# Twelve convolution blocks of a hybrid layer move from a filler stream into Winograd pairs

## The chip, the cores and the metric

The kernel runs on one core of one Trainium2 chip. The metric is the time of one execution on the device in microseconds (us). Times of several executions are given as a median with the lowest and the highest; the profile and the trace come from one further execution, whose own time is given with them.

## The reference, cut to what matters

One step of a one-layer encoder. A prompt of 1024 tokens and a sample of 64 tokens are treated together as T = 1088 columns. All projections of the first half come from one weight matrix; `[z | xBC | dt | q | k | v | g_ssm | g_att]` are its outputs.

```python
proj = _rmsnorm(x) @ w_in
z, xbc, dt, q, k, v, g_ssm, g_att = split(proj)
xbc = silu(causal_conv4(past, xbc) + bias)      # 4 taps per channel, 3072 channels
x_s, B, C = split(xbc)                          # 2048 + 4*128 + 4*128
y_s = ssd_scan(x_s, dt, B, C) ...               # 4 groups of 8 heads
o = diff_attention(q, k, v)                     # 8 heads, two softmaxes each
x += W_out(sig(g_ssm) * (y_s @ W_bs) + sig(g_att) * (o @ W_ba))
x += conv_ffn(rmsnorm(x))
```

The change concerns `xbc`: a projection from 1024 to 3072 channels, a causal convolution of width 4 along the tokens of each channel, and silu. In the kernel it is 24 blocks of 128 channels. Block f = 16 + g holds B of state-space group g, block 20 + g its C, and blocks 4g to 4g + 3 its x.

## The kernel before, in words

Every float32 product is made of three TensorE products of rounded parts: `w_hi * b_hi`, `w_hi * b_lo` and `w_lo * b_hi`. Activations lie as 128 channels (partitions) by tokens; a matmul takes a 128x128 weight part and 272 tokens (a quarter of T).

The stages, in order of time:

1. **Values and parts.** The input is normalised and split into high and low parts.
2. **Input pairs** (`in_pair`, L646, listed in `INPUT`, L81). Two weight blocks at a time are multiplied with Winograd's form of Strassen's scheme: the two blocks' 256 channels and the 1024 inputs and 1088 tokens are cut in two each way, and seven products of half size take the place of eight. Each product p is made for two column halves s, so a pair has 14 *steps* (p, s) of 4 k-parts times 3 matmuls, 12 matmuls each, 168 in all. Here 20 pairs run: q and k (4 pairs each), z (8) and four of the gate pairs. `pile` issues a step's matmuls into a PSUM bank; the result is read by ScalarE (`S.copy`, L698 and L708) or VectorE (additions of partial sums, L700, L702, L710), and `done` finishes a quarter (a quarter is 128 channels by 544 tokens, named by block r and token half c) with silu (z, L676), tanh or nothing (gates) or squares (q, k) and stores it. The seven weight parts of the *next* pair are made beside it: loads of four quarters, four additions on GpSimd (L573 to L579) and seven splits into high and low (`split`, a cast on ScalarE L429 and a subtraction on VectorE L430), at steps that `lefts_at` lists.
3. **Side jobs beside the pairs.** `take_turn` is called once in each step; it advances a list of generators, `running`, and starts new ones from `beside`: cached keys, the step sizes dt, and finishing of q and k (norm, rotation, splits). A count of its turns puts the end of the last of these jobs at step 5 of the 15th pair.
4. **Attention with a filler stream** (from about 560 us to 1112 us). 72 units `attend` (8 heads of 9 row blocks) each do score matmuls S (L1128, L1129), the maximum on VectorE (L1133, L1137), two exponentials on ScalarE (L1142), the subtraction of the two softmaxes on VectorE (L1144 to L1146), transposes T on TensorE (L1157), copies (L1162, L1164) and the product with the values (L1177). Between a unit's transposes and its value products, `fill(rate)` (L1041) takes work from the generator `stream` (L1028): plain blocks, `project` (L178), each of 4 column parts of 24 matmuls (8 k-parts times 3, L171 to L173), 96 matmuls in all. `ORDER` (L80) lists them: 24 convolution blocks (`conv_tiles`, L987) and 8 gate blocks. The filler is counted in portions of 363 columns; a column part counts 272/363 = 0.75 portions, a block 3.0. `fill(FIRST)` takes 4 portions before the first unit, and each unit takes `ATT_STEPS` = 1.12 portions more. What is left over, and then the branch products, is taken in the scan.
5. **Scan** of the state-space groups, with filler; then the branches, the output and the feed-forward half, which the change does not touch.

In `conv_tiles` the two column parts of a token half are copied from PSUM to `pre` (L1002), with three columns ahead of them for the past (GpSimd copies, L997, L999, L1004, L1013, L1014); ScalarE makes tap 0 with bias (L1017), VectorE the three others (L1019); tanh (L1020) and one more VectorE operation (L1021) make silu, since tanh shares a function table with the softmax's exponential. The result goes to `x_sc` in device memory (L1022), which the scan reads.

The order of instructions on each engine is made by a scheduler when the kernel is built: it takes the ready instruction that is earliest in the program, `tc.high_priority` lifts some, and `after(...)` or `tc.issue_after` forbids one to come before another. On the chip each engine then runs its list in order. PSUM has 8 banks: in the input pairs 7 of them take products in turn, in attention 2 take filler (`pm`), 4 scores and 2 transposes.

Of the kernel before, what the change touches and what calls it, by code (L numbers as in the profile page):

```python
# [9 lines left out]
F32 = mybir.dt.float32  # L10
R32 = mybir.dt.float32r
AF = mybir.ActivationFunctionType
ALU = mybir.AluOpType
# [4 lines left out]
P = 128  # L18
D = 1024
KT = D // P  # L20
TP, TS = 1024, 64
T = TP + TS
PAST = 512
WIDE = ((0, 384), (384, 384), (768, 320))
HT = T // 2
# [42 lines left out]
LAST = 200  # L68
FIRST = 4
IDLE = 12  # L70
ATT_STEPS = 1.12
SCAN_STEPS = 1.17
BRANCH_AT = 2

# [1 line left out]
def group(g):  # L76
    return 16 + g, 20 + g, *range(4 * g, 4 * g + 4)


ORDER = (("c", group(0)), ("g", (11, 10)), ("c", group(1)), ("g", (9, 8)), ("c", group(2)), ("c", group(3)), ("g", (3, 2)))  # L80
INPUT = [(k, i) for k in "qk" for i in range(4)] + [("z", i) for i in range(8)] + [("g", i) for i in (2, 3, 6, 7)]  # L81
Q_DONE = 3

O_MIX, O_FFN, O_CW, O_CB, O_SN, O_D = 0, 8, 16, 112, 136, 152
# [6 lines left out]
def hybrid_layer(ctx: ExitStack, tc: tile.TileContext, xT, xt, prm, cst, rope, wvd, win, wbs, wba, wout, wup, wdn,  # L91
# [32 lines left out]
    def col(o):  # L124
        return par[:, o : o + 1]
# [36 lines left out]
    def after(*names):  # L162
        pins = ExitStack()
        for n in names:
            pins.enter_context(tc.issue_after(seen[n].ins))
        return pins
# [316 lines left out]
    rows_l = tc.alloc_tile_pool(name="rl", bufs=1)  # L483
    rows_r = tc.alloc_tile_pool(name="rg", bufs=1, side="right")

    def row(tag, name, dt=F32):
        if tag in ("fa", "fs", "fu"):
            w = {"fa": KT * P, "fs": 4 * P, "fu": HT}[tag]
            return rows_l.tile([P, w], dt, name=name, tag=tag, bufs=IN_ROWS[tag])
        w = {"ss": T}.get(tag, HT)  # L490
        return rows_r.tile([P, w], dt, name=name, tag=tag, bufs=IN_ROWS[tag])

    def couple(t, n=2):
        return t[:, : n * QW].rearrange("p (a t) -> p a t", a=n)
# [124 lines left out]

    def blocks_of(n):  # L620
        kind, j = INPUT[n]
        return [win[FIRST_BLOCK[kind] + 2 * j + r] for r in range(2)]

    def plain_left(n):
# [21 lines left out]
    def in_pair(n):  # L646

        kind, j = INPUT[n]
        u1, u2 = row("fx" if n == 1 else "fu", "u1"), row("fu", "u2")
        banks, out = {}, {}  # L650

        def pile(key, p, s, start):
            if start:
                banks[key, s] = acc(W2[s])
            ps, w, b = banks[key, s], left[n][p], parts[PARTS[p], s]
            for k in range(4):
                c = slice(P * k, P * (k + 1))
                for i, (x, y) in enumerate(((0, 0), (0, 1), (1, 0))):
                    seen["mm"] = PE.matmul(ps, w[x][:, c], b[y][:, k], start=start and k == i == 0, stop=k == 3 and i == 2,
                                           skip_group_check=not start)  # L660
            return ps

        def to(r, c, s):

            if (r, c) not in out:
                out[r, c] = row("fp", "pre")
            a, w = O2[s], W2[s]
            return out[r, c][:, a : a + w]

        def done(r, c):  # L670
            cs = slice(HT * c, HT * (c + 1))
            t = out[r, c][:, :HT]
            f = 2 * j + r
            if kind == "z":
                with after("root"):
                    seen["silu"] = act(t, t, AF.Silu)  # L676
            elif kind == "g":
                if f >= KT:
                    act(t, t, AF.Tanh, scale=0.5)
            else:  # L680
                if kind not in squares:
                    squares[kind] = row("ss", "ss")
                ss = squares[kind][:, cs]
                if (kind, c) not in begun_squares:
                    begun_squares.add((kind, c))
                    act(ss, t, AF.Square)
                else:
                    sq = row("fc", "sq")[:, :HT]
                    act(sq, t, AF.Square)
                    V.tensor_tensor(out=ss, in0=ss, in1=sq, op=ALU.add)  # L690
            send(out={"z": z_sc, "q": q_r, "k": k_r, "g": g_sc}[kind][P * f : P * (f + 1), cs], in_=t)

        at = yield
        for _ in range(14):
            p, s = at
            us = cols(s)
            if p == 0:
                seen["copy"] = S.copy(u1[:, us], pile("a", p, s, True))  # L698
            elif p == 1:
                seen["read"] = V.tensor_tensor(out=u2[:, us], in0=pile("b", p, s, True), in1=u1[:, us], op=ALU.add)  # L700
            elif p == 3:
                seen["read"] = V.tensor_tensor(out=u1[:, us], in0=pile("b", p, s, False), in1=u1[:, us], op=ALU.add)  # L702
            else:
                r, c, key, start, u = {2: (0, 0, "a", False, None), 4: (1, 1, "c", True, u1), 5: (1, 0, "d", True, u1),
                                       6: (0, 1, "c", False, u2)}[p]
                ps = pile(key, p, s, start)
                if u is None:
                    seen["copy"] = S.copy(to(r, c, s), ps)  # L708
                else:
                    seen["read"] = V.tensor_tensor(out=to(r, c, s), in0=ps, in1=u[:, us], op=ALU.add)  # L710
                if s == 1:
                    ripe.append(lambda r=r, c=c: done(r, c))
            at = yield
# [1288 lines left out]
```

## Time and profile before

| | |
|---|---|
| median of 3 executions | 2408.86 us (2404.99 to 2409.06) |
| profiled execution: its time, its span | 2400.86 us, 2399.1 us |
| TensorE busy (matmuls), granted clock | 99% of the span, 0.998 |
| VectorE, ScalarE, GpSimd busy | 72%, 50%, 26% |

How to read the lines: PE is TensorE's matmuls and PEld its weight loads, DVE is VectorE, ACT ScalarE, POOL GpSimd, SP the engine that issues most DMAs. A line such as `L1019 DVE SCALAR_TENSOR_TENSOR cc<-pre,par,cc` is line 1019 of the kernel on VectorE writing tile `cc` from `pre`, `par` and `cc`; behind it stand the count, busy microseconds, the mean in nanoseconds, and idle time of the engine ahead of it with what ended it. A PE duration includes the pipeline, so the distance from start to start, not the duration, is what a matmul costs. A row of the window view gives the stretch, its length, and each engine's busy time (with the number of instructions).

### The profile page before, as it was taken

Reading aid. Unit: us, or ns where it says so; the run is one execution under the profiler, and the core shown is the slowest. Engines: PE = TensorE matmul, PEld = TensorE weight load, DVE = VectorE, ACT = ScalarE, POOL = GpSimd, SP = SyncE. Lnnn points to the kernel's source line nnn. Section 1 sums busy time; section 2 is a strip of 40 time slices with the busy share of each in tenths; the row PEclk is TensorE's granted clock in tenths of the full one; section 3 lists DMA queues with packets and bytes.
Section 4 is the critical chain, followed back from the end, with each engine's and each line's share of the span. In section 5 each row is a group of like instructions: output and inputs, shape, how many; then the busy total and the mean of one; then the engine's idle time right before and its main releaser. Section 6 shows DMA issues by size and latency. Waiting matters only on the chain.

```text
span 2399.1 us, 48662 instructions
## 1 busy us (share of the span) xinstructions
PE 2376.1 (99%) x18661; PEld 2306.1 (96%) x18661; DVE 1725.5 (72%) x2953; ACT 1197.8 (50%) x2592; POOL 623.0 (26%) x683
## 2 busy tenths in 40 slices
PE   9999999999999999999999999999999999999999
PEld 9999999999999999999899889999999999999999
DVE  4678987646858768884789886646866766767866
ACT  6344454425656656665666674334533443353432
POOL 0032444220100000001222220013254554453343
PEclk9999999999999999999999999999999999999999
DMA  7873868426555444435988956664124424357975
GB/s 248 273 243 135 275 214 310 165 105 205 158 160 161 148 141 138 143 114 183 360 272 287 333 192 207 197 211 139 63 82 159 148 96 160 124 182 220 253 189 120
DMA packets 288202, 450.58 MB, mean 188 GB/s; under 512 B 35865, under 2 KB 178082, under 8 KB 287970
## 3 DMA queue, kind: packets, MB, share of 16 engines
q1 hardware_dynamic: 259058, 388.39, 49.0%
q0 software_dynamic: 10176, 25.50, 5.0%
q10 hardware_dynamic: 18736, 33.59, 3.9%
q8 instruction: 147, 2.41, 0.4%
q14 instruction: 85, 0.70, 0.1%
HBM read 294.86 MB, written 152.50 MB: 186 GB/s over the span
## 4 chain that ended last, share of the span: by engine, by line
PE 56%; DVE 3%; DMA 1%; issue 1%; ACT 1%; SPq 0%; DVEq 0%; ACTq 0%
PE mx L1639 13%; PE mx L1821 6%; PE mm L1639 5%; PE mm L171 4%; PE mm L173 4%; PE mm L172 4%; PE mx L173 3%; PE mx L171 3%; PE mx L172 3%; PE mm L1821 2%; PE yi L1328 1%; PE stp L1340 1%; PE ye L1334 1%; PE po L1177 1%; PE tr L1307 1%
## 5 line engine op out<-in xcount | busy, mean ns | idle before, releaser
L171 PE MATMUL mm<-b,w_hi 128*128 128x272 f32 x1376 | 409.2, 297 | 0.0
L173 PE MATMUL mm<-b,w_lo 128*128 128x272 f32 x1376 | 404.0, 294 | 0.0
L172 PE MATMUL mm<-b,w_hi 128*128 128x272 f32 x1376 | 403.8, 294 | 0.0
L171 PEld LDWEIGHTS mm<-b,w_hi 128*128 128x128 f32 x1376 | 259.4, 188 | 7.2 <-issue 4.9
L172 PEld LDWEIGHTS mm<-b,w_hi 128*128 128x128 f32 x1376 | 259.4, 189 | 6.2 <-issue 4.9
L173 PEld LDWEIGHTS mm<-b,w_lo 128*128 128x128 f32 x1376 | 258.9, 188 | 3.9 <-issue 3.1
L1639 PE MATMUL mx<-m,w_hi 128*128 128x272 f32 x776 | 149.3, 290 | 1.5 <-ACT m L429 1.3
L430 DVE TENSOR_TENSOR wh<-w_f,wh 128x512 fp32r<-128x512 f32 (+1 forms) x156 | 149.1, 956 | 0.0
L1639 PE MATMUL mx<-n,wh 128*128 128x272 f32 x1056 | 141.2, 288 | 1.2 <-DVE u L1666 1.2
L1639 PEld LDWEIGHTS mx<-n,wh 128*128 128x128 f32 x1056 | 135.7, 188 | 1.4 <-DVE u L1666 1.4
L1142 ACT ACTIVATE p_t<-sc,mx 128x512 f32<-128x512 f32 (+6 forms) x144 | 106.0, 739 | 58.7 <-DVE mx L1133 35.0
L171 PE MATMUL mx<-b,w_hi 128*128 128x272 f32 x416 | 122.5, 295 | 1.6 <-ACT w_hi L156 1.1
L1639 PEld LDWEIGHTS mx<-m,w_hi 128*128 128x128 f32 x776 | 121.9, 188 | 2.0 <-ACT m L429 1.5
L172 PE MATMUL mx<-b,w_hi 128*128 128x272 f32 x416 | 122.0, 294 | 0.0
L173 PE MATMUL mx<-b,w_lo 128*128 128x272 f32 x416 | 120.1, 291 | 0.2 <-DVE w_lo L157 0.2
L573 POOL TENSOR_TENSOR ws<-w_f 128x512 f32<-128x512 f32 (+1 forms) x51 | 69.2, 1356 | 195.0 <-DMA w_f<-in_win_dram 94.0
L1019 DVE SCALAR_TENSOR_TENSOR cc<-pre,par,cc 128x544 f32<-128x544 f32 (+1 forms) x144 | 111.2, 772 | 8.2 <-ACT cc L1017 6.9
L157 DVE TENSOR_TENSOR w_lo<-w_f,w_hi 128x1024 fp32r<-128x1024 f32 (+1 forms) x74 | 91.1, 1232 | 31.3 <-ACT w_hi L156 30.7
L1639 PE MATMUL mx<-m,w_lo 128*128 128x272 f32 x388 | 112.0, 289 | 0.0
L1648 ACT ACTIVATE cc<-pre,par 128x544 f32<-128x544 f32 (+1 forms) x44 | 37.2, 845 | 148.0 <-DVE pre L1683 147.0
L429 ACT CAST wh<-w_f 128x512 fp32r<-128x512 f32 (+1 forms) x156 | 95.3, 613 | 28.7 <-POOL w_f L579 7.9
L156 ACT CAST w_hi<-w_f 128x1024 fp32r<-128x1024 f32 (+1 forms) x74 | 77.5, 1049 | 51.5 <-PE mm L172 28.4
(472 smaller groups left out, 7123.4 us busy)
## 6 DMA issues: line engine op xcount, KB each, us to landing
w_f<-in_win_dram SPq DMA_DIRECT2D x40, 512.0 KB, 3.6
w_f<-in_wup_dram SPq DMA_DIRECT2D x80, 256.0 KB, 2.6
w_f<-in_win_dram SPq DMA_DIRECT2D x76, 256.0 KB, 3.2
bc<-a_sc SPq DMA_DIRECT2D x32, 512.0 KB, 6.7
b<-y_sc SPq DMA_DIRECT2D x24, 544.0 KB, 9.3
h_sc<-hb SPq DMA_DIRECT2D x44, 272.0 KB, 2.1
ht<-h_sc SPq DMA_DIRECT2D x22, 544.0 KB, 4.7
t_sc<-ht SPq DMA_DIRECT2D x22, 544.0 KB, 2.9
```

The source lines that it names most:

```text
L156: S.copy(hi, w)
L157: V.tensor_tensor(out=lo, in0=w, in1=hi, op=ALU.subtract)
L171: PE.matmul(ps, a_hi, b_hi, start=i == 0, stop=False)
L172: PE.matmul(ps, a_hi, b_lo, start=False, stop=False)
L173: PE.matmul(ps, a_lo, b_hi, start=False, stop=i == n - 1)
L429: S.copy(hi, src)
L430: V.tensor_tensor(out=lo, in0=src, in1=hi, op=ALU.subtract)
L573: G.tensor_tensor(out=s1, in0=q21, in1=q22, op=ALU.add)
L1019: V.scalar_tensor_tensor(cc[:, :m], pre[:, i : i + m], cw(i), cc[:, :m], ALU.mult, ALU.add)
L1142: act(p_t[:n, :nk], sc[c][:n, :nk], AF.Exp, bias=mx[:n, c : c + 1], accum_out=dst)
L1639: PE.matmul(ps, w[x][:, c], b[y][:, k], start=start and k == i == 0, stop=k == 3 and i == 2, skip_group_check=not start)
L1821: PE.matmul(ps, w[y][:, c], b[z][:, k], start=start and k == j == 0, stop=k == n - 1 and j == 2, skip_group_check=not start)
```

## The change

The twelve convolution blocks of state-space groups 0 and 1 leave the filler stream and become six input pairs, two blocks each (`PAIRED`): (B0, C0), two pairs of x of group 0, and the same for group 1. They stand between the last six pairs of `INPUT` (z 6, z 7, gates 2, 3, 6, 7), one before each; the number of pairs goes from 20 to 26. The stream keeps groups 2 and 3 and the gates: 20 blocks instead of 32, and `ATT_STEPS` goes from 1.12 to 0.62.

In such a pair the quarters are written to `fx` rows (550 wide now instead of 544, as are the `fc` rows) behind three free columns; the last part of the second token half is written in two pieces around the sample's own past. When a quarter is there, `done` starts a generator `convolved` on `running`: a GpSimd memset or four small GpSimd copies and tap 0 on ScalarE in one turn, one VectorE tap in each of the next three, silu (ScalarE's Silu, with a scale of 2 since the taps' weights are halved) in the next, and in the next the store. The second token half of a block needs the first one's last columns, so (r, c) = (1, 1) waits for (1, 0) and starts three turns after it.

```diff
-ATT_STEPS = 1.12
+ATT_STEPS = 0.62
...
-ORDER = (("c", group(0)), ("g", (11, 10)), ("c", group(1)), ("g", (9, 8)), ("c", group(2)), ("c", group(3)), ("g", (3, 2)))
-INPUT = [(k, i) for k in "qk" for i in range(4)] + [("z", i) for i in range(8)] + [("g", i) for i in (2, 3, 6, 7)]
+PAIRED = ((16, 20), (0, 1), (2, 3), (17, 21), (4, 5), (6, 7))
+ORDER = (("c", group(2)), ("g", (11, 10)), ("c", group(3)), ("g", (9, 8)), ("g", (3, 2)))
+INPUT = [(k, i) for k in "qk" for i in range(4)] + [("z", i) for i in range(6)]
+INPUT += [x for i, y in enumerate([("z", 6), ("z", 7)] + [("g", j) for j in (2, 3, 6, 7)]) for x in (("c", i), y)]
...
+        w = {"ss": T, "fx": HT + 6, "fc": HT + 6}.get(tag, HT)
...
+            if kind == "c" and c == 1 and s == 1:
+                m = TP - HT - a
+                return [(0, out[r, c][:, d + a : d + a + m]), (m, out[r, c][:, d + a + m + 3 : d + a + w + 3])]
...
+        def convolved(r, c):
+            t, f = out[r, c], PAIRED[j][r]
+            n, m = (HT, HT) if c == 0 else (TP - HT, HT + 3)
+            if c == 0:
+                G.memset(t[:, 0:3], 0.0)
+            else:
+                G.tensor_copy(t[:, 0:3], out[r, 0][:, HT : HT + 3])
...
+            cc = row("fc", "cc", more=True)
+            with after("copy"):
+                act(cc[:, :m], t[:, :m], AF.Identity, bias=col(O_CB + f), scale=cw(0))
+            yield 1
+            for i in range(1, 4):
+                with after("read"):
+                    V.scalar_tensor_tensor(cc[:, :m], t[:, i : i + m], cw(i), cc[:, :m], ALU.mult, ALU.add)
+                yield 1
+            with after("root", "copy"):
+                seen["silu"] = act(cc[:, :m], cc[:, :m], AF.Silu, scale=2.0)
+            yield 1
+            rs = slice(P * f, P * (f + 1))
+            send(out=x_sc[rs, HT * c : HT * c + n], in_=cc[:, :n])
...
+            if kind == "c":
+                for x in {(0, 0): (0,), (1, 0): (0, 1), (0, 1): (1,), (1, 1): ()}[r, c]:
+                    running.append([1 + 3 * (r == 1 and x == 1), convolved(r, x)])
+                return
```

## The prediction on record

> **What bounds the kernel now.** I read the page first, then the window view cut at the stages that the change touches, then single pairs and single attention units in the timeline, and last what TensorE's transposes wait for.
>
> ```profile
> PE 2376.1 (99%) x18661; PEld 2306.1 (96%) x18661; DVE 1725.5 (72%) x2953; ACT 1197.8 (50%) x2592; POOL 623.0 (26%) x683
> ```
>
> ```profile
> core 0: us, PE busy (x) PEld busy (x) DVE busy (x) ACT busy (x) POOL busy (x), PEclk, DMA share, GB/s
> 1200.00:1300.00 100.00, 100.00 (x830) 90.51 (x829) 89.54 (x126) 65.23 (x154) 26.68 (x20) 1.00 0.77 261
> 380.00:440.00 60.00, 59.59 (x471) 59.13 (x471) 48.15 (x84) 27.21 (x53) 21.87 (x23) 1.00 0.85 285
> 560.00:1112.00 552.00, 550.10 (x4224) 527.49 (x4222) 413.07 (x817) 336.62 (x866) 43.39 (x120) 1.00 0.46 146
> 443.00:548.00 105.00, 105.00 (x836) 105.00 (x835) 44.81 (x83) 34.65 (x66) 22.15 (x18) 1.00 0.33 116
> ```
>
> ```profile
> L1157 PE MATMUL pt<-con,p_t x328: 221/272/329, 580.3 to 1108.3; 128*128 128x128 f32 x144, 64*128 64x64 f32 x16, 64*64 64x64 f32 x4
> ...
> its engine sat idle before it (us, times) until:
>   issue: 1.7, 9
>   PE sc L1128: 0.7, 2
> ```
>
> TensorE is the bound everywhere, at full granted clock: 1.9 us idle in 552 us of attention (third row), none in the last five light pairs (fourth row), and the 328 transposes of attention, asked what they wait for, name no other engine. So a matmul that goes away is time, as long as nothing else ends later. The fourth row also shows room beside a light pair: VectorE is busy for 44.8 of 105 us. The first two rows are the measure for a crowded VectorE: 89.5% and 80% busy, with TensorE idle for 0 of 100 and 0.4 of 60 us.
>
> **Matmuls removed and added.** The distance from start to start, in two light pairs and in a piece of filler inside attention:
>
> ```profile
> 460.27 0.42 PE L659 MATMUL mm<-t,w_hi 128*128 128x272 f32 x2
> ...
> 481.43 0.42 PE L659 MATMUL mx<-t,w_hi 128*128 128x272 f32 x2
> ...
> 502.58 0.42 PE L659 MATMUL mx<-t,w_hi 128*128 128x272 f32 x2
> ```
>
> ```profile
> 810.91 0.29 PE L171 MATMUL mm<-b,w_hi 128*128 128x272 f32 x1
> ...
> 813.17 0.29 PE L171 MATMUL mm<-b,w_hi 128*128 128x272 f32 x1
> ```
>
> A pair of 168 matmuls takes 21.15 us, 125.9 ns each. In the filler, 18 matmuls lie between the two starts: 2.26/18 = 0.1256 us. Twelve plain blocks are 12 x 96 = 1152 matmuls, 1152 x 0.1259 = 145.0 us out of attention; six pairs are 6 x 168 = 1008, 6 x 21.15 = 126.9 us into the input stage. The balance is 144 matmuls, **-18.1 us**. The counts are fixed by the code, so that the change might save no matmuls is no case. The Trainium skill, page "TensorE: Matmul & The Clock Gate", section "Back-to-back issue gap", gives an isolated gap of columns/2.4 + 2.5 ns, 115.8 ns for 272 columns; by it the balance would be an estimated 16.7 us. The trace's 125.9 ns decides.
>
> Nothing is pushed on into the scan. Before, 32 blocks of 3.0 portions less 4 less 72 x 1.12 leave 11.36 portions; after, 20 x 3.0 - 4 - 72 x 0.62 leave 11.36 too.
>
> **Attention with less cover.** It goes from 552 to 407 us, a unit from 552/72 = 7.67 to 5.65 us. This is where the gain can be lost: the way from a unit's first score to its transposes through VectorE and ScalarE was covered by filler, and 45% of the filler's rate goes. One of the tightest units and a loose one (head 3, rows 7 and 1):
>
> ```profile
> 770.17 0.40 PE L1128 MATMUL sc<-kh,q 128*128 128x512 f32 x1
> ...
> 778.23 1.28 DVE L1146 SCALAR_TENSOR_TENSOR p_t<-p_t,sm 128x1024 f32<-128x1024 f32 x1
> ...
> 782.11 0.60 PE L1157 MATMUL pt<-con,p_t 128*128 128x128 f32 x4
> ```
>
> ```profile
> 795.64 0.28 PE L1128 MATMUL sc<-kh,q 128*128 128x256 f32 x1
> ...
> 800.76 0.42 DVE L1146 SCALAR_TENSOR_TENSOR p_t<-p_t,sm 128x256 f32<-128x256 f32 x1
> ...
> 810.17 0.38 PE L1157 MATMUL pt<-con,p_t 128*128 128x128 f32 x2
> ```
>
> The first needs 779.51 - 770.17 = 9.3 us of the 11.9 until TensorE turns to it, 2.6 to spare; the second 5.5 of 14.5, 9.0 to spare. Read so, the 72 units have 6.9 us to spare on average and 1.1 at least. If every interval shrinks by 5.65/7.67 = 0.74 and no chain gets shorter, 11 units are late, by 10.0 us together. That is the dear end. The cheap end is 0: the convolution leaves the same queues. Its VectorE work:
>
> ```profile
> L1019 DVE SCALAR_TENSOR_TENSOR cc<-pre,par,cc 128x544 f32<-128x544 f32 (+1 forms) x144 | 111.2, 772 | 8.2 <-ACT cc L1017 6.9 <-issue 0.2
> ...
> L1021 DVE SCALAR_TENSOR_TENSOR cc<-pre,cc 128x544 f32<-128x544 f32 (+1 forms) x48 | 34.3, 715 | 5.2 <-ACT pre L1020 5.1
> L157 DVE TENSOR_TENSOR w_lo<-w_f,w_hi 128x1024 fp32r<-128x1024 f32 x28 | 34.2, 1220 | 14.3 <-ACT w_hi L156 14.0
> ```
>
> Half of the first two rows and 12 of the 28 splits are 55.6 + 17.2 + 14.7 = 87.4 us, so VectorE has 325.7 of 407 us, 80% where it had 75%, under the 89.5% that the scan bears. ScalarE, even with nothing taken from it, would have 336.6 of 407, 83%. I take **+2 us**, near the cheap end, because the order puts a transpose where it is ready and filler elsewhere; a longer list of late units would show as idle time of TensorE ahead of L1157.
>
> **The six pairs beside TensorE.** Their queues:
>
> ```profile
> L676 ACT ACTIVATE pre<-pre 128x544 f32<-128x544 f32 x32 | 21.0, 658 | 21.4 <-DVE pre L710 17.3 <-DMA w_f<-in_win_dram 2.4 <-ACT xh L786 1.3
> L1648 ACT ACTIVATE cc<-pre,par 128x544 f32<-128x544 f32 x22 | 18.6, 845 | 0.9 <-DVE m L430 0.9
> L1187 ACT ACT_TABLE_LOAD x7 | 9.0, 1283 | 0.1
> ```
>
> ```profile
> 464.65 0.33 ACTq L691 DMA_DIRECT2D z_sc<-pre  x1
> ```
>
> ```profile
> z_sc<-pre ACTq DMA_DIRECT2D x32, 272.0 KB, 3.9
> ```
>
> Of a light pair, a weight addition on GpSimd, an addition and a split on VectorE, and the shortest, median and longest of twelve such splits:
>
> ```profile
> 469.20 1.30 POOL L575 TENSOR_TENSOR w_f<-w_f,ws 128x512 f32<-128x512 f32 x1 [9.51 <-issue]
> ```
>
> ```profile
> 469.54 0.44 DVE L710 TENSOR_TENSOR pre<-mx,u 128x272 f32<-128x272 f32 x1 [0.47 <-PE mx L659]
> 469.90 1.16 DVE L430 TENSOR_TENSOR wh<-w_f,wh 128x512 fp32r<-128x512 f32 x1
> ```
>
> ```profile
> L430 DVE TENSOR_TENSOR wh<-w_f,wh x12: 681/684/1159, 462.3 to 533.4; 128x512 fp32r<-128x512 f32 x12
> ```
>
> - VectorE: a pair has 44.81 x 21.15/105 = 9.0 us. A convolution pair and the light one behind it have 18.0 + 12 taps x 0.772 = 27.3 us in 42.3. Nine of the twelve taps fall from step 13 to step 4 of the light pair; in its steps 1 to 3 six taps (4.6 us), two splits (1.4) and two additions (0.9) meet 4.5 us, a lag of 2.4 us. Seven PSUM banks at 1.5 us a step hide that; bare, it costs 6 x 2.4 = 14 us.
> - ScalarE: 14.0 us for the two plus 4 x (0.845 + 0.658) = 20 us in 42.3. The 36 stores, six a pair, go through its queue, 0.33 us each. Silu and the tanh of gates 6 and 7 change tables at most six times, 7.7 us over the last 85. Off the path: 0.
> - `fc` has three buffers and a pair fills four: the fourth tap 0 waits for the first store. From store to that tap are four steps, 6.0 us, against 3.9 to land. If it comes late ScalarE stands with the two copies that free `pile`'s first banks queued behind: about 2 us a pair, 12 in all.
> - GpSimd, 22.15 of 105 us, gets a few copies of three columns; tap 0, and ScalarE's queue behind it, wait if they queue behind a weight addition (1.3 us). Up to 1.3 us four times a pair, covered like the VectorE lag.
> - The last side job ends at step 5 of the 15th pair, now the first of the six, and shares `fx`: one landing, 3.9 us, once.
>
> I take 0 for all of these, by the 380 to 440 row (VectorE at 80% and a quarter of GpSimd's time taken, 0.4 us lost); the dear end is some 12 us.
>
> **Sum.** -18.1 + 2 = -16.1 us: the profiled execution's 2400.86 becomes 2384.8. That execution was 8.0 us under the median of the runs; from the median the same sum gives 2392.8. I forecast 2391, nearer the median, which is the metric.
>
> **Rivals.** *Attention becomes bound by its chain (slower).* Should the intervals shrink to 0.65 of now, as when units without filler of their own follow big ones, 19 units are late by 25.6 us: 2408.9 - 18.1 + 25.6 = 2416. It decides from 0.69, where the lateness reaches 18.1. For it speak the rows of unit 7 above; against it 6.9 us of spare time on average, and chains without taps in their queue. Chance 0.10.
>
> *The pairs stall (no change).* If each of the six loses two steps, 3.0 us, to the late tap 0 or the lag of the evacuations, the 18.1 us are gone: 2409. For it speaks ScalarE's strict order, against it the 380 to 440 row. Chance 0.07.
>
> *Taps and GpSimd block each other (less gain).* The split that meets the weight addition of 469.20 takes 1159 ns where the median has 684; the addition just ahead of it, which reads PSUM, stays at 0.44 us. A tap also reads two SBUF tiles. If each of the eight additions of two pairs held one tap for all its 1.3 us, VectorE would have 27.3 + 10.4 = 37.7 of 42.3 us: not a bound, but a lag that can cost two microseconds a pair, 12 us: 2402.8. Chance 0.05. The Trainium skill, page "SBUF — State Buffer", section "Who interferes with whom", says that a VectorE instruction with two SBUF inputs and a GpSimd one that reads SBUF take turns on one read interface, the later one fully blocked; the rows agree.
>
> **How the numbers follow.** The forecast has 0.78. A measurement here can tell about 0.2%, 4.8 us, from no change. Forecast and blocking are faster by more, 0.83; stalling pairs the same, 0.07; the chain slower, 0.10. The range reaches from 2383 (2400.9 - 18.1) to 2403 (2408.9 - 18.1 + 12), and leaves out the two rivals with 0.17.
>
> **What would show it.** Right: 26 pairs at 21.15 us, no idle time of TensorE in the last 254 us of them, attention at about 409 us, VectorE at about 80% in it, TensorE some 18 us less busy over the span. Wrong: idle time ahead of L1157 or L1177 that VectorE or ScalarE ends (the chain), a pair above 23 us or idle time ahead of `pile` that ends with ScalarE or VectorE (stalls), taps far above 0.8 us (blocking).

## The result, and the profile after

| | before | after |
|---|---|---|
| median (lowest to highest, 4 runs each, same chip) | 2408.96 us (2404.99 to 2409.62) | 2429.37 us (2428.23 to 2433.54) |
| ratio, 95% interval | | 1.0091 [1.0074, 1.0109] |
| profiled execution: time, span | 2400.86, 2399.1 us | 2428.23, 2426.4 us |

The change makes the kernel slower by 0.9%, some 20 us; the forecast was 18 us faster. The page of after, first TensorE's line:

```profile
PE 2369.0 (98%) x18517; PEld 2292.2 (94%) x18517; DVE 1755.1 (72%) x3031; ACT 1199.0 (49%) x2586; POOL 655.3 (27%) x707
```

The count went from 18661 to 18517: the 144 matmuls are saved. Now the window view of after over the last eleven of the twelve pairs in which new and light ones alternate (each stretch, its length, then each engine's busy time):

```profile
core 0: us, PE busy (x) PEld busy (x) DVE busy (x) ACT busy (x) POOL busy (x), PEclk, DMA share, GB/s
443.00:548.00 105.00, 105.00 (x837) 105.00 (x836) 75.69 (x128) 47.95 (x87) 38.06 (x51) 1.00 0.32 107
548.00:680.00 132.00, 132.00 (x1051) 132.00 (x1050) 85.33 (x150) 52.88 (x96) 38.27 (x50) 1.00 0.32 110
```

TensorE stands still for nothing in 237 us. The last pair's matmul ends at 680.7 us, before at 554.1: 126.6 us for six pairs, forecast 126.9. So the pairs do what was said. The rest was lost behind them. The window view, cut at the last matmul of the pairs, the last value product of attention and the last product `yi` of the scan; first before, then after:

```profile
554.10:1112.00 557.90, 556.00 (x4271) 533.33 (x4269) 414.74 (x819) 338.15 (x868) 43.39 (x120) 1.00 0.47 148
1112.00:1461.00 349.00, 349.00 (x2847) 314.48 (x2847) 284.51 (x377) 221.04 (x535) 84.90 (x68) 1.00 0.83 280
```

```profile
680.70:1133.50 452.80, 427.11 (x3177) 397.81 (x3175) 329.50 (x712) 276.11 (x752) 21.57 (x60) 1.00 0.50 155
1133.50:1485.70 352.20, 345.27 (x2812) 309.88 (x2810) 287.62 (x379) 219.49 (x533) 85.93 (x68) 1.00 0.83 277
```

In attention TensorE is idle for 452.80 - 427.11 = 25.7 us where it was 1.9, in the scan for 6.9 where it was 0.0. To compare stages with different filler, the filler is taken out: its first matmul of each three (L171 before, L173 after) by the window view of that line alone, for attention, scan and all that follows:

```profile
554.10:1112.00 557.90, 271.32 (x925) 174.15 (x924) 1.00 0.47 148
1112.00:1461.00 349.00, 169.57 (x555) 104.55 (x555) 1.00 0.83 280
1461.00:2399.00 938.00, 164.95 (x568) 106.89 (x568) 1.00 0.53 160
```

```profile
680.70:1133.50 452.80, 164.94 (x560) 105.75 (x559) 1.00 0.50 155
1133.50:1485.70 352.20, 163.95 (x544) 102.33 (x544) 1.00 0.83 277
1485.70:2426.00 940.30, 163.38 (x560) 106.52 (x560) 0.99 0.53 159
```

The sums are 2048 and 1664; the difference is 384, three matmuls each: the 1152 that left. At the forecast's 0.126 us a matmul, 0.378 a count, **attention less its filler** is 557.9 - 925 x 0.378 = 208.3 us before and 452.8 - 560 x 0.378 = 241.1 after. The same sum gives 139.2 and 146.6 for the scan and 723.3 and 728.6 for what follows. So the change of the span comes apart into

126.6 (pairs) - 145.2 (1152 filler matmuls) + 32.8 (attention) + 7.4 (scan) + 5.3 (what follows) = 26.9 of 27.3 us.

Before's profiled execution was 8 us under its median; medians give +20.4. As the experiments show, that execution was some 7 us short in scan and what follows, so against an ordinary execution of before these two lose nearer 6 us together than 13. Attention's 33 us are the result; 23.8 of them are added idle time of TensorE.

What TensorE waits for in attention, by the view of the costliest groups for TensorE, between 555 and 1112 us of before and then between 681 and 1134 us of after (busy, mean ns, then idle time ahead and what ended it):

```profile
L1177 PE MATMUL po<-v_t,a_t 128*128 128x128 f32 (+1 forms) x592 | 81.4, 275 | 0.0
L1128 PE MATMUL sc<-kh,q 128*128 128x512 f32 (+4 forms) x208 | 69.6, 342 | 0.6 <-ACT p_t L1142 0.5
...
L1157 PE MATMUL pt<-con,p_t 128*128 128x128 f32 (+2 forms) x328 | 52.4, 269 | 0.0
```

```profile
L1218 PE MATMUL po<-v_t,a_t 128*128 128x128 f32 (+1 forms) x592 | 83.5, 278 | 8.7 <-ACT a_t L1203 4.5 <-DVE a_t L1205 4.2
L1169 PE MATMUL sc<-kh,q 128*128 128x512 f32 (+4 forms) x208 | 72.0, 351 | 9.8 <-ACT p_t L1183 9.6
...
L1198 PE MATMUL pt<-con,p_t 128*128 128x128 f32 (+2 forms) x328 | 53.8, 273 | 6.7 <-DVE ol L1247 3.8 <-ACT po L1220 2.8
```

Value products (L1218) wait for the copy of the transposes out of PSUM, scores (L1169) for a bank that an exponential has yet to read, transposes (L1198) for one of the two banks they share with value products and output transposes. The subtraction of the softmaxes (L1187), on which the prediction's price rested, is not among them: 6.6 of the 6.7 us ahead of L1198 are ended by `ol` and `po`. One such place in the timeline, TensorE first, then VectorE:

```profile
935.92 0.62 PE L1198 MATMUL pt<-con,p_t 128*128 128x128 f32 x4
937.06 0.55 PE L1198 MATMUL pt<-con,p_t 128*128 128x128 f32 x3 [0.52 <-DVE ol L1247]
938.55 1.69 PE L1218 MATMUL po<-v_t,a_t 128*128 128x128 f32 x13 [0.95 <-DVE a_t L1205]
```

```profile
936.26 0.74 DVE L1247 SCALAR_TENSOR_TENSOR ol<-pt,wcol,oh 128x512 fp32r<-128x512 f32 x1
936.92 0.77 DVE L1060 SCALAR_TENSOR_TENSOR cc<-pre,par,cc 128x547 f32<-128x547 f32 x1
...
937.74 0.67 DVE L1205 COPY a_t<-pt 128x512 f32<-128x512 f32 x1
```

Four transposes, then 0.52 us until `ol` has been read out of the second bank, three transposes, then 0.95 us until the copy of the first four (512 columns), which stands behind a tap on VectorE, is done. There is no filler matmul in this stretch; filler ran from 929 to 935 us, just ahead of it.

A wait can cost more than itself. After one of 2.44 us the granted clock drops to 0.50 for 3.4 us, from 1082.7 us on; the two filler matmuls below, six apart, lie 1.36 us from each other, 0.227 us a matmul where it is 0.126 at the full clock. Below them stands the window view of these 3.4 us, with the clock third from its end:

```profile
1081.17 0.39 PE L1169 MATMUL sc<-kh,q 128*128 128x256 f32 x1 [2.44 <-ACT p_t L1183]
...
1083.02 0.43 PE L173 MATMUL mm<-b,w_hi 128*128 128x272 f32 x1
...
1084.38 0.43 PE L173 MATMUL mm<-b,w_hi 128*128 128x272 f32 x1
```

```profile
1082.70:1086.10 3.40, 3.40 (x17) 3.40 (x17) 1.92 (x6) 0.50 (x3) 0.00 (x0) 0.50 0.00 0
```

At that pace nearly half of the 3.4 us is lost, an estimated 1.5. Of attention's 33 us some 5 more are the ends of the matmuls just ahead of the waits: their records count whole as busy, 0.27 us on average, where a matmul in line costs about 0.11. The last 2 or 3 us are not traced.

### The profile page after: what moved, and what is told of

Same layout as the page of the kernel before. It is cut to its first block, busy times and chain, and to the rows that moved or that the text cites. A ratio compares the mean times of both kernels' runs of the same rounds, so it can differ in the third digit from the quotient of the medians.

```text
span 2426.4 us, 48427 instructions
## 1 busy us (share of the span) xinstructions
PE 2369.0 (98%) x18517; PEld 2292.2 (94%) x18517; DVE 1755.1 (72%) x3031; ACT 1199.0 (49%) x2586; POOL 655.3 (27%) x707
## 5 line engine op out<-in xcount | busy, mean ns | idle before, releaser
L173 PE MATMUL mm<-b,w_hi 128*128 128x272 f32 x1000 | 297.3, 298 | 0.0
L174 PE MATMUL mm<-b,w_hi 128*128 128x272 f32 x1000 | 294.9, 295 | 0.0
L175 PE MATMUL mm<-b,w_lo 128*128 128x272 f32 x1000 | 294.8, 295 | 0.0
L174 PEld LDWEIGHTS mm<-b,w_hi 128*128 128x128 f32 x1000 | 189.0, 189 | 5.6 <-issue 4.5
L173 PEld LDWEIGHTS mm<-b,w_hi 128*128 128x128 f32 x1000 | 188.8, 189 | 5.3 <-issue 3.8
L175 PEld LDWEIGHTS mm<-b,w_lo 128*128 128x128 f32 x1000 | 188.6, 189 | 4.9 <-issue 4.3
L432 DVE TENSOR_TENSOR wh<-w_f,wh 128x512 fp32r<-128x512 f32 (+1 forms) x174 | 161.0, 926 | 0.1
L576 POOL TENSOR_TENSOR ws<-w_f 128x512 f32<-128x512 f32 (+1 forms) x57 | 79.3, 1390 | 232.0 <-DMA w_f<-in_win_dram 122.1
L173 PE MATMUL mx<-b,w_hi 128*128 128x272 f32 x408 | 121.4, 298 | 1.7 <-ACT grs L1406 1.7
L664 PE MATMUL mx<-t,w_hi 128*128 128x272 f32 x624 | 119.9, 289 | 0.6 <-DVE t L432 0.6
L431 ACT CAST wh<-w_f 128x512 fp32r<-128x512 f32 (+1 forms) x174 | 106.2, 614 | 27.7 <-POOL w_f L582 6.0
L664 PE MATMUL mx<-t,wh 128*128 128x272 f32 x816 | 111.2, 290 | 0.9 <-ACT wh L431 0.9
L578 POOL TENSOR_TENSOR w_f<-w_f,ws 128x512 f32<-128x512 f32 (+1 forms) x57 | 80.7, 1416 | 104.0 <-issue 56.8
```

The source lines that it names most:

```text
L173: PE.matmul(ps, a_hi, b_hi, start=i == 0, stop=False)
L174: PE.matmul(ps, a_hi, b_lo, start=False, stop=False)
L175: PE.matmul(ps, a_lo, b_hi, start=False, stop=i == n - 1)
L431: S.copy(hi, src)
L432: V.tensor_tensor(out=lo, in0=src, in1=hi, op=ALU.subtract)
L576: G.tensor_tensor(out=s1, in0=q21, in1=q22, op=ALU.add)
```

## The experiments

**How many pairs.** Three kernels move only the first two, three or four pairs; the other blocks stay in the stream, and the rate leaves the same rest for the scan. The fourth keeps all six and issues a unit's value products one unit later, just ahead of the next unit's transposes, so that a fill and the next scores stand between a unit's transposes and its products.

```diff
-ATT_STEPS = 0.62
+ATT_STEPS = 0.953   # 0.87, 0.787
-ORDER = (("c", group(2)), ...
+ORDER = (("c", (2, 3)), ("g", (11, 10)), ("c", (17, 21, 4, 5, 6, 7)), ("g", (9, 8)), ("c", group(2)), ...
-... for x in (("c", i), y)]
+... for x in ((("c", i), y) if i < 2 else (y,))]
```

```diff
             while len(waiting) > n:
                 unit, done = waiting.pop(0)
+                multiply()
                 next(unit)
+                turned.append((unit, done))
                 with tc.issue_after(seen["scores"].ins):
                     fill(rate)
-                run(unit)
...
```

> Only the first two convolution pairs (group 0's B and C and its first x pair) are made; the other 20 convolution blocks stay in the filler, at 0.953 portions a unit so that the same remainder is left for the scan. Theory one, attention lacks cover and loses more than in proportion: TensorE saves 6.0 us and attention and scan lose at most 4, so 0 to 6 us under the kernel before, about 2405. Rival, each pair costs a fixed amount wherever it is (45.9 us of loss over six pairs, 7.6 a pair, against 3.0 saved): 9 us over the kernel before, about 2418.

> The first three pairs (group 0 complete), rate 0.87. Theory one (cover): saves 9.0, loses 3 to 10, so within 6 us under to 1 over the kernel before. Rival (fixed cost a pair): 14 us over it, about 2423.

> The first four pairs, rate 0.787. Theory one (cover): saves 12.1, loses 10 to 20, so 0 to 8 us over the kernel before. Rival (fixed cost a pair): 18 us over it, nearly as slow as the change with all six.

> The change with all six pairs, but a unit's value products stand one unit later in the program, just ahead of the next unit's transposes, so that the copies of the transposes are long done when TensorE comes to the products. If the way from transposes through their copies to the products is what has lost its cover (TensorE waits 9.1 us there in the changed kernel), 8 to 15 us less than the change, about 2417. Rival, the score banks and exponentials set the pace and the wait only moves: within 4 us of the change, the time ahead of the scores growing by what the products lose.

The table holds these and the later runs that vary the rate. "Less filler" is each stage's time less 0.126 us for each filler matmul in it, counted matmul by matmul, which differs from the sums above by some tenths. The ratio is to the kernel before on the same chip.

| kernel | pairs moved, portions a unit | attention less filler (idle), us | scan, what follows less filler | median us, ratio [95%] |
|---|---|---|---|---|
| before | 0, 1.12 | 208.7 (1.9) | 139.1, 723.3 | |
| two pairs | 2, 0.953 | 211.9 (3.7) | 149.5, 731.0 | 2418.68, 1.0046 [1.0031, 1.0061] |
| three pairs | 3, 0.87 | 222.3 (9.9) | 149.0, 733.9 | 2427.27, 1.0080 [1.0064, 1.0096] |
| four pairs | 4, 0.787 | 225.0 (11.1) | 149.7, 728.2 | 2424.01, 1.0071 [1.0054, 1.0088] |
| after, 0.66 | 6, 0.66 | 231.5 (17.1) | 150.1, 731.8 | 2423.25, 1.0068 [1.0051, 1.0084] |
| after | 6, 0.62 | 241.4 (25.7) | 146.6, 729.0 | 2429.37, 1.0091 [1.0074, 1.0109] |
| before, 0.62 | 0, 0.62 | 243.5 (24.9) | 177.1, 733.1 | 2484.44, 1.0322 [1.0307, 1.0338] |
| after, 0.56 | 6, 0.56 | 243.7 (24.9) | 145.9, 729.6 | 2429.67, 1.0093 [1.0078, 1.0108] |
| products later | 6, 0.62 | 238.6 (21.8) | 147.9, 730.7 | 2430.90, 1.0098 [1.0083, 1.0113] |

The loss in attention grows with what is taken out of it: 3 us for two pairs, 14, 16 and 33 for three, four and six. It isn't in step with the pairs, as a fixed cost of each would be. But two pairs are slower too, and there it isn't attention: scan and what follows lose some 10 and 8 us against the profile of before, which neither theory had. Products issued later change little: their idle time falls, attention gains 2.8 us and the time nothing. So the copies that end the wait ahead of L1218 are not the cause by themselves.

Differences of a few microseconds between these rows carry the clock too. In attention the trace has it at 0.50 for no time in before and with two pairs, for 3.4 us in after, and for 10.2 us both in the kernel before at 0.62 and with products later; by the same estimate these two lose some 3 us more there than after.

**Edits that save nothing.** Is scan and what follows slower after any edit? One run takes 0.01 portions a unit from the kernel before, one swaps two of its light pairs, and a later one is the kernel after with no pair moved.

```diff
-ATT_STEPS = 1.12
+ATT_STEPS = 1.11
```

```diff
-... [("z", i) for i in range(8)] ...
+... [("z", i) for i in (0, 1, 2, 3, 4, 5, 7, 6)] ...
```

```diff
-PAIRED = ((16, 20), (0, 1), (2, 3), (17, 21), (4, 5), (6, 7))
+PAIRED = ()
...
-ATT_STEPS = 0.62
+ATT_STEPS = 1.12
```

> The kernel before with the filler rate of attention 1.11 instead of 1.12, no pair moved: 0.72 portions, 2.9 us of TensorE work, pass from attention to the scan. Theory A (the order of the scan and of what follows is fitted to the kernel's own stream, and any edit ahead of it loses): scan and the part behind it lose 8 to 15 us, attention at most 3; time 2416 to 2423. Rival B (the loss of scan and tail comes from something that the moved pairs bring): within 3 us of the kernel before, 2406 to 2412.

> The kernel before with z pairs 6 and 7 in the other order; the same work in the same stages. Theory A (any edit ahead of the scan loses there): 2416 to 2423, with the loss in the scan and behind it, not in attention. Rival B (moved pairs are the cause): within 3 us of the kernel before.

> The kernel after with no pair moved: 20 pairs, 32 blocks in the stream, 1.12 portions a unit, only the rows of two tags six columns wider. Theory layout (wider rows move every buffer behind them, and the order found for scan and tail is another): scan and what follows lose 6 to 13 us, time 2413 to 2420. Theory pairs (what was moved causes it): within 4 us of the kernel before, 2403 to 2411.

They gave 2407.14 (ratio 1.0000 [0.9989, 1.0010]), 2408.90 (0.9998 [0.9984, 1.0012]) and 2410.16 us (1.0009 [0.9998, 1.0020]): no loss. The theory that any edit loses falls, and so does the one of the wider rows. The window view of the last of them, attention and scan:

```profile
559.40:1116.50 557.10, 555.91 (x4270) 533.30 (x4269) 414.74 (x819) 338.11 (x868) 43.23 (x120) 1.00 0.48 148
1116.50:1467.90 351.40, 349.56 (x2848) 314.58 (x2848) 285.30 (x377) 221.20 (x535) 84.49 (x68) 1.00 0.83 279
```

This execution of the same work has its scan at 351.4 us, not 349.0. In the three, scan less filler is 141.4 to 143.2 us and what follows 726.3 to 728.0, where the profile of before had 139.1 and 723.3. Against these the kernel after loses 3 to 5 us in the scan and 1 to 3 behind it, two to four pairs 6 to 8 and up to 8. That smaller loss comes with the moved pairs or with the thinner rate, which these runs do not part; it is made of waits of 0.2 to 3.8 us (loads of x_sc, the gates' scales, a state) and of the clock: after stands 3.4 us ahead of the scan's last `gst`, and the clock is then at 0.50 for 6.8 us, which before and these three don't have there. Its cause stays open.

**The rate alone.** Two runs change the rate of the kernel after, one gives the kernel *before* after's rate.

```diff
-ATT_STEPS = 0.62
+ATT_STEPS = 0.66    # 0.56; in the kernel before: 1.12 to 0.62
```

> The kernel after with 0.66 portions a unit for 0.62: 2.9 portions, 11.6 us of TensorE work, go from the scan into attention. Theory cover (the loss in attention is the filler that is missing between a unit's transposes and its products): attention's time less its filler falls by 3 to 6 us from 241.4, TensorE's idle time there from 25.7 to about 20, the scan loses less than that; time 2421 to 2428. Rival (attention's length is set by another engine's work or by a fixed order, whatever the rate): attention grows by 11.6 us with its filler, less filler stays the same within 2 us, time within 3 us of the kernel after.

> The kernel after with 0.56 portions a unit for 0.62: 4.3 portions, 17.4 us of TensorE work, go from attention into the scan. Theory cover: attention's time less its filler grows by 4 to 8 us from 241.4, and its idle time from 25.7 to about 32; the scan, with more filler, gives back at most 3; time 2431 to 2437. Rival: attention shrinks by the 17.4 us of its filler, less filler it stays the same within 2 us; time within 3 us of the kernel after.

> The kernel before, no pair moved, with 0.62 portions a unit in attention instead of 1.12: 36 portions, 145 us of TensorE work, go from attention into the scan and behind it; nothing is saved. Theory cover (attention loses because a unit has 0.62 portions, wherever the other blocks went): attention's time less its filler rises from 208 to 238-245 us as in the kernel after; the scan has filler in plenty and gives back at most 3; time 2430 to 2445. Rival (the loss comes with the pairs: their late stores, another order of blocks, other tables): attention less its filler stays under 220, time under 2420.

The last one decides. The view of the groups for its TensorE in attention, no pair moved:

```profile
L1177 PE MATMUL po<-v_t,a_t 128*128 128x128 f32 (+1 forms) x592 | 84.3, 280 | 7.4 <-DVE a_t L1164 4.0 <-ACT a_t L1162 3.2
L1128 PE MATMUL sc<-kh,q 128*128 128x512 f32 (+4 forms) x208 | 72.4, 353 | 9.8 <-ACT p_t L1142 9.6
...
L1157 PE MATMUL pt<-con,p_t 128*128 128x128 f32 (+2 forms) x328 | 54.2, 275 | 6.7 <-DVE ol L1206 3.8 <-ACT po L1179 2.8
```

It is after's list but for 1.3 us ahead of the value products, and attention less filler is 243.5 us against after's 241.4. So the thin rate alone, with no pair moved, makes the whole loss in attention; the pairs, their stores and tables add nothing to it that these 2 us could show. The time itself missed what was expected by 40 us, for a reason of its own. The window view of its attention and scan:

```profile
554.90:1009.40 454.50, 429.59 (x3173) 400.05 (x3171) 335.40 (x720) 277.32 (x755) 23.63 (x67) 0.99 0.51 154
1009.40:1403.30 393.90, 371.06 (x2909) 329.94 (x2908) 347.00 (x445) 275.54 (x626) 114.95 (x121) 0.97 0.67 224
```

The scan, which now holds the convolution blocks, has VectorE at 347.0 of 393.9 us, 88%, and TensorE idle for 22.8 us; less filler it lost 38 us. The granted clock of that row is 0.97, an estimated 11 or 12 of these. With 0.66 attention gained 9.9 us, more than cover was expected to give, and the scan lost 3.5 of it; the time fits. With 0.56 attention lost 2 us, not 4 to 8, and the time is after's, as the rival had it: at these two rates the loss has levelled off.

**Lumps.** Filler comes in column parts of 0.75 portions, so at 0.62 some units have none. Counted along TensorE's list, 21 groups of value products follow their transposes with no filler between (the expectations say 23), 3 before, and the 8.7 us stand there. Two runs hand out half parts:

```diff
-            product_over(ps, w_hi, w_lo, rows_of)
+            for k in range(KT):
...
+                if k == KT // 2 - 1:
+                    yield w / 2
...
-            yield w
+            yield w / 2
...
```

> The kernel after, with the filler handed out in half column parts (12 matmuls, 0.375 portions) instead of whole ones (24, 0.75), the same rate. Theory bare units (0.62 portions in lumps of 0.75 leave some units with no matmul between their transposes and their value products: 23 such places after, 3 before, and all of TensorE's 8.7 us ahead of value products stand there): places without filler fall under 12, idle time ahead of value products under 4 us, attention less its filler from 241.4 to 228-236; time 2417 to 2426. Rival (the average rate decides, the lumps don't): the idle time moves to scores and transposes, attention less its filler within 4 us of 241, time 2426 to 2433.

> The kernel after with half column parts and 0.66 portions a unit together. Theory bare units: attention less its filler 222 to 230 us, time 2413 to 2421. Rival (rate alone): as with 0.66 alone, 231.5 us less filler and 2420 to 2427.

2435.30 us (1.0116 [1.0097, 1.0135]) and 2427.67 (1.0086 [1.0065, 1.0106]); attention less filler 244.4 and 234.7 us. The edit didn't do what it was made for: the places without filler rose to 29, so the theory of bare units isn't tested as meant. But it has little left: more such places came with less idle time ahead of value products (8.7 to 4.7 us), while that ahead of transposes rose from 6.7 to 9.6. The 3 us that attention lost are no more than the clock's: it was at 0.50 for 13.6 us there.

**Whose queue.** Four runs change who copies the transposes, two in after, one in before and one in after with 0.66 portions; a fifth leaves out the stream's taps on VectorE.

```diff
-                    if (i + b0 // 4) % 2:
-                        S.copy(m3(a4, full), m3(pt, full))
-                    else:
-                        V.tensor_copy(m3(a4, full), m3(pt, full))
+                    V.tensor_copy(m3(a4, full), m3(pt, full))   # or S.copy
```

```diff
                 act(cc[:, :m], pre[:, :m], AF.Identity, bias=col(O_CB + f), scale=cw(0))
-                for i in range(1, 4):
-                    V.scalar_tensor_tensor(cc[:, :m], pre[:, i : i + m], cw(i), cc[:, :m], ALU.mult, ALU.add)
```

> The kernel after, with all copies of transposed probabilities on VectorE (half of them were on ScalarE). Theory exponentials (ScalarE's queue sets the pace: scores wait for banks that an exponential has yet to read): idle time ahead of scores falls from 9.9 to under 5 us and attention less its filler by 5 us or more, time 2419 to 2425. Theory cover (any chain is late for lack of filler, VectorE's too): idle time ahead of scores falls, that ahead of value products and transposes grows as copies queue behind the maxima; attention less its filler within 4 us of 241 or above, time 2427 to 2436.

> The kernel after, with the full copies of transposed probabilities all on ScalarE (the 56 on VectorE were 29.7 us). Theory VectorE's queue (in the stretches where TensorE waits VectorE works without a pause, taps between maxima and copies): attention less its filler falls from 241.4 to 228-236 us, time 2416 to 2425. Rival latency (the chain from scores to products is as long on an idle engine, the queues don't matter): within 4 us of 241, time 2426 to 2433. Rival ScalarE: it grows by 8 us or more, as exponentials stand behind the copies.

> The kernel after without the three VectorE taps of the stream's twelve convolution blocks, 72 instructions and some 55 us of VectorE; the output of these blocks lacks them. Theory VectorE's queue: attention less its filler falls from 241.4 to 215-228 us, time 2400 to 2416. Rival latency: within 5 us of 241, time 2424 to 2433.

> The kernel before with the copies on ScalarE. Theory cover (with 1.12 portions a unit the chain's length is hidden, so a shorter one gains nothing): within 3 us of the kernel before, attention less its filler 207 to 210 us. Rival (the copies' place is worth something by itself): 4 us or more faster.

> The kernel after with the copies on ScalarE and 0.66 portions a unit. If the two gains add (9 us in attention each, 6 given back by the scan for the rate): attention less its filler 221 to 226 us, time 2412 to 2418. If both cure the same waits: 227 to 232 us and 2418 to 2424.

| kernel | attention less filler (idle), us | VectorE busy in attention | median us, ratio [95%] |
|---|---|---|---|
| after | 241.4 (25.7) | 329.5 | 2429.37, 1.0091 [1.0074, 1.0109] |
| copies on VectorE | 257.0 (35.8) | 349.4 | 2448.05, 1.0175 [1.0158, 1.0191] |
| copies on ScalarE | 232.3 (15.9) | 306.5 | 2420.87, 1.0060 [1.0041, 1.0080] |
| no taps in the stream | 237.3 (19.3) | 289.4 | 2430.50, 1.0100 [1.0079, 1.0120] |
| copies on ScalarE, 0.66 | 224.2 (11.7) | | 2428.92, 1.0085 [1.0064, 1.0105] |
| before, copies on ScalarE | 208.2 (1.1) | | 2412.08, 1.0015 [1.0002, 1.0027] |

The groups of TensorE in attention, with the copies on VectorE and then on ScalarE:

```profile
L1215 PE MATMUL po<-v_t,a_t 128*128 128x128 f32 (+1 forms) x592 | 86.5, 283 | 7.8 <-DVE a_t L1202 6.9 <-ACT pre L1061 0.8
L1169 PE MATMUL sc<-kh,q 128*128 128x512 f32 (+4 forms) x208 | 72.9, 355 | 14.2 <-ACT p_t L1183 13.4 <-DMA q<-q_st 0.7
...
L1198 PE MATMUL pt<-con,p_t 128*128 128x128 f32 (+2 forms) x328 | 54.4, 275 | 8.9 <-DVE ol L1244 7.2 <-ACT po L1217 1.7
```

```profile
L1215 PE MATMUL po<-v_t,a_t 128*128 128x128 f32 (+1 forms) x592 | 85.0, 282 | 4.5 <-ACT a_t L1202 3.0 <-DVE ol L1244 1.4
L1169 PE MATMUL sc<-kh,q 128*128 128x512 f32 (+4 forms) x208 | 72.0, 350 | 7.2 <-ACT p_t L1183 7.2
...
L1198 PE MATMUL pt<-con,p_t 128*128 128x128 f32 (+2 forms) x328 | 53.3, 272 | 3.6 <-ACT po L1217 2.5 <-ACT a_t L1202 0.7 <-DVE ol L1244 0.4
```

A wait is named after the engine that ended it, and that name alone misleads here: scores wait for ScalarE's exponentials, yet work taken *off* ScalarE makes that wait longer (9.8 to 14.2 us) and work put on it makes it shorter (7.2). The place of the copies is worth 16 us the one way, far more than either theory had, and 9 the other. VectorE's load as such is worth less: 40 us less of it, without the taps, takes 6.4 us of idle time and 4 us in all out of attention (the clock, at 0.50 for 13.6 us there, takes some back) and nothing out of the time. And where cover is full, the copies on ScalarE give nothing (208.2 us; the time, 5 us longer, is just outside the 3 us expected). So with thin filler TensorE feels how long a handful of handovers takes. In the timelines, from the start of a group's last transpose to the end of its copy, the 112 groups of attention take 1.20 us on average in before, 1.33 in after, 1.44 with all copies on VectorE and 1.11 with the full ones on ScalarE: in line with the maxima and subtractions a copy comes later than in line with the exponentials. The taps hardly delay it: the copies that stay on VectorE take 1.35 us in after and 1.32 without taps. So of the two theories, VectorE's queue fits the copies alone, and latency the taps alone. With 0.66 the two gains add in attention (17 us), but scan and what follows give 13 us back (153.8 and 735.1), and the time is after's. No version here beat the kernel before.

## Why the prediction was wrong

- **Matmuls removed and added** was right: 144 fewer, 126.6 us for six pairs where 126.9 were forecast.
- **The six pairs beside TensorE** was right with its 0: no idle time in 237 us. Stalling pairs, the rival with no change, did not come. Some taps did get slower, as the third rival had it, without a microsecond of TensorE's. The view of VectorE's groups between 443 and 680 us of after has them at 899 ns, against 772 for those of the stream before, but the view of their line shows the median at 782:

```profile
L695 DVE SCALAR_TENSOR_TENSOR cc<-pre,par,cc 128x544 f32<-128x544 f32 (+1 forms) x71 | 61.8, 899 | 0.2
```

```profile
L695 DVE SCALAR_TENSOR_TENSOR cc<-pre,par,cc x72: 772/782/1846, 440.8 to 669.3; 128x544 f32<-128x544 f32 x36, 128x547 f32<-128x547 f32 x36
```

Nine of the 72 took 1.1 to 1.85 us, and each of these began while a GpSimd weight addition ran; the other 63 took 0.77 to 0.79. The Trainium skill, page "SBUF — State Buffer", section "Who interferes with whom", lets such a VectorE instruction and one of GpSimd take turns on a read interface; the nine agree. No run here moved the additions away.

- **Attention with less cover** is the step that failed: +2 us, with a dear end of 10.0; measured 33. Not the size alone was off. The prediction watched one chain, from the scores to the transposes, and found 6.9 us to spare. It let every interval from first score to first transpose shrink to 0.74 with the filler; they grew. Read in the same way, the 72 intervals of after are 19.5 us on average where they were 14.4, and leave 10.1 us to spare on average and 1.7 at least: the scheduler's new order puts the scores further ahead. The unit of head 3, row 7, which had 2.6 us to spare, has 865.55 - 856.80 = 8.7:

```profile
847.25 0.40 PE L1169 MATMUL sc<-kh,q 128*128 128x512 f32 x1
...
855.52 1.28 DVE L1187 SCALAR_TENSOR_TENSOR p_t<-p_t,sm 128x1024 f32<-128x1024 f32 x1
...
865.55 0.60 PE L1198 MATMUL pt<-con,p_t 128*128 128x128 f32 x4
```

So no unit's transposes came late by that chain, and L1187 ends none of the waits listed ahead of L1198. What came late were handovers that the prediction didn't price at all, because before they show no idle time: transposes to copy to value products (8.7 us), exponentials to the next scores (9.8), and the turn of two PSUM banks (6.7). "The order puts a transpose where it is ready and filler elsewhere" held for the transposes' own chain. It didn't help the short handovers: at the place shown above the filler had all run just before them. Why the order found is this one stays open.
- **Its measure of room** was wrong too: "under the 89.5% that the scan bears". VectorE had 329.5 of 452.8 us, 73%, and TensorE lost 25.7. The kernel before at 0.62 has a scan at 88% that lost 22.8, where a stretch of the same stage at 89.5% had lost nothing. A share says nothing of who waits at a handover.
- **Nothing is pushed on into the scan** was right in portions and wrong as a zero: some 6 us, measured against the median of before, are lost in the scan and behind it.
- **The slower rival** had the sign and, by luck, much of the size (2416, a loss of 25.6 us in attention), but by another mechanism: 19 late units, where none was late; its chance of 0.10 came from that chain's 6.9 us to spare. What this case offered and the prediction didn't use: at 1.12 portions a unit TensorE was idle for 1.9 us in attention, so the profile of before couldn't show what cover was worth, either way. The cost of 45% less of it should have been bounded by all handovers of a unit, not by the longest.

From the median: -18.1 + 33 + 6 = +21; measured +20.4.

## What to carry to other kernels

Filler that keeps a matmul engine busy beside a chain has two values: its work, and the waits that it covers; work moved elsewhere at a profit of 18 us cost 33 us of cover. Before a plan thins filler out, run the *old* kernel with the thin rate and look at the one stage: that run separates the loss of cover from everything else in the change, even where its whole time tells nothing. And where the waits sit on several short handovers, curing one (products later, half lumps, taps away) took at most 6.4 us of idle time away here and nothing from the time: part of it moved to the next, and part went into the clock that drops after a wait.

## What the runs showed that was not expected

The engine that ends a wait need not be the one to relieve: scores waited 9.8 us for exponentials on ScalarE, 14.2 with less work on ScalarE, 7.2 with more. Behind many waits of some 2 us the granted clock was 0.50 for 3.4 us or a multiple of it, an estimated 1.5 us more for each 3.4. And one profiled execution can lie 8 us beside its median: before's scan and what follows, less filler, were together 862.4 us, and 868.9 to 869.6 in three executions of other kernels with all but the same work.
